# Both float32r parts of the input projection weights kept in DRAM from the first pass over the tokens

## The chip, the cores and the metric

The kernel runs on one core of one Trainium2 chip. The metric is device time in microseconds (us) from start to end of one execution. The core has a matrix engine (PE, with its weight loads PEld), a vector engine (DVE), an activation engine (ACT), GpSimd (POOL), a queue engine (SP) that issues most transfers, and 16 DMA engines that all queues share.

## What is computed

One layer of a hybrid encoder on 2112 tokens (2048 of a prompt, 64 of a running stream) of width 1024. All operands are float32.

```python
h    = rms_norm(x)
proj = einsum('btd,dc->btc', h, w_in)          # 1024 -> 5376 columns
A    = (bg * conv3_causal(cg * xin)) @ w_conv_out           # from the first 1536 columns
B    = rwkv7(proj[..., 1536:3328]) @ w_rwkv_out             # recurrence over tokens, state per head
m    = sigmoid(gate_A) * A + sigmoid(gate_B) * B            # gates: the last 2048 columns
x    = x + rms_norm(m @ w_o)
x    = x + rms_norm(swiglu(rms_norm(x)))
```

## The kernel before

Tokens lie on the free axis, features on the 128 partitions. Phase A does the input projection and the RWKV-7 recurrence; after it come the merge of the branches and the feed-forward part, which the change does not touch.

The projection's 5376 columns are 42 blocks of 128 (`w_in[c]`, 128x1024 floats, 512 KB each). The tokens are four quarters of 528, each done as two halves of 264. `PASSES` lists the work: a first pass with all 42 blocks for quarter 0, then passes with 28 blocks (quarter 1), 30 blocks (quarter 2) and 42 blocks (quarter 3), and at the end the 14 + 12 gate blocks that quarters 1 and 2 left over. So 168 units are done, and each block is fetched four times.

A float32 product is done as three float32r products: weights and activations are each split into a high part (rounded to float32r) and a low part (the rest), and `mm3` adds hi*hi, hi*lo and lo*hi. A unit takes 2 x 24 matmuls of 264 columns. Its weights come from `weights`: SP loads the block into `w_raw` (2 buffers), ACT writes `w_hi` (3 buffers) as a cast, DVE writes `w_lo` (3 buffers) as `w_raw - w_hi`. The load of the next unit is asked for at the start of a unit (`need`). ACT, DVE and SP each run their instructions strictly in the order written.

Between the projection's matmuls lie the three streams of the recurrence (`scan_prep`, `scan_solve`, `scan_chain`), which work on groups of 128 tokens: small matmuls, some 62 short DVE instructions per group that solve a triangular system (the tiles `tm`, `ti`, `al`), and round trips through DRAM (`asc`, `ttsc`). Two more jobs share the engines in phase A: `weight_sums`, which loads blocks of the feed-forward weights (`sw`), adds them on DVE and stores the sums (`us_s`, `ds_s`) for later, and the norm of the next quarter. A scheduler at build time sets the order in which each engine's instructions stand; it may bring a transfer forward where its queue would stand idle.

Of the kernel before, what the change touches and what calls it, by code (L numbers as in the profile page):

```python
# [16 lines left out]
P = 128  # L17
# [11 lines left out]
KT = D // P  # L29
# [56 lines left out]
class Trunk:  # L86
# [27 lines left out]
    def scratch(self):  # L114
        d = self.dram
        self.lo_s = d.tile([12, P, T], F32, name="lo_s")
        self.sg_s, self.a_s, self.g_s = self.lo_s[0:4], self.lo_s[4:8], self.lo_s[8:12]
        for nm in ("r", "v", "bv"):
            setattr(self, nm + "_s", d.tile([4, P, T], F32, name=nm + "_s"))
        self.ks_s = d.tile([12, P, T], F32, name="ks_s")  # L120
        self.gt_s = d.tile([16, P, T], F32, name="gt_s")
        self.cv_s = d.tile([4, P, T], F32, name="cv_s")
        self.yr_s = d.tile([4, P, T], F32, name="yr_s")
        self.x1_s = d.tile([KT, P, T], F32, name="x1_s")
        self.ds_s = d.tile([4, 4, P, FH * P], F32, name="ds_s")
        self.us_s = d.tile([4, NF, P, HK * P], F32, name="us_s")
        self.nb_s = d.tile([2, len(DOWN), HK, P, FB], F32, name="nb_s")
# [14 lines left out]
    def weights(self, src, kt=KT):  # L142

        nc = self.nc
        raw = self.wp.tile([P, KT, P], F32, name="w_raw", bufs=2)
        hi = self.wp.tile([P, KT, P], F32R, name="w_hi", bufs=WBUFS)
        lo = self.wp.tile([P, KT, P], F32R, name="w_lo", bufs=WBUFS)
        nc.sync.dma_start(out=raw[:, :kt], in_=src)
        nc.scalar.copy(out=hi[:, :kt], in_=raw[:, :kt])  # L149
        nc.vector.tensor_tensor(out=lo[:, :kt], in0=raw[:, :kt], in1=hi[:, :kt].bitcast(F32), op=ALU.subtract)  # L150
        return hi, lo

    def mm3(self, ps, w, r, kts, rk0=0, first=True, last=True, **kw):

# [122 lines left out]
        self.summing, self.sum_wait = self.weight_sums(), 24  # L277
        self.lora_in, self.conv_u, self.kf, self.bn = {}, {}, {}, {}

    def project(self, w, h, n):  # L280

        ps = self.mmps()
        for k in range(0, KT, KSTEP):
            if k:
                self.side_step()
                yield
            self.mm3(ps[:, :n], w, h, range(k, k + KSTEP), rk0=k, first=k == 0, last=k + KSTEP == KT)
        return ps

    def rwkv_unit(self, q, j, c, w, h):  # L290
# [3 lines left out]
        if 4 <= c < 8:  # L294
            a = pool.tile([P, NB], F32, name="ka", bufs=2)[:, :n]
            nc.sync.dma_start(out=a, in_=self.a_s[m, :, t0:t0 + n])
        ps = yield from self.project(w, h, n)
        x = pool.tile([P, NB], F32, name="psv", bufs=4)
        pr = pool.tile([P, NB + 2], F32, name="pr", bufs=2)
        for b, (s0, sn, sample) in enumerate(segments(t0, n)):  # L300
# [147 lines left out]
    def conv_unit(self, q, j, c, what, w, h):  # L448
        pool, nc = self.pa, self.nc
        t0, n = halves(q)[j]  # L450
        ps = yield from self.project(w, h, n)
        if what == 0:
            u = self.conv_u[j] = pool.tile([P, NB + 4], F32, name="u", bufs=2)
            for b, (s0, sn, sample) in enumerate(segments(t0, n)):
                b = s0 + 2 * b
                nc.scalar.copy(out=u[:, b + 2:b + 2 + sn], in_=ps[:, s0:s0 + sn])
        elif what == 1:
            u = self.conv_u[j]
            for b, (s0, sn, sample) in enumerate(segments(t0, n)):
                hist = self.u_hist_s if sample else self.u_hist  # L460
                b = s0 + 2 * b
                nc.gpsimd.tensor_copy(out=u[:, b:b + 2], in_=hist[:, c, :])
                nc.vector.tensor_tensor(out=u[:, b + 2:b + 2 + sn], in0=ps[:, s0:s0 + sn], in1=u[:, b + 2:b + 2 + sn], op=ALU.mult)
                nc.gpsimd.tensor_copy(out=hist[:, c, :], in_=u[:, b + sn:b + sn + 2])
        else:
            u = self.conv_u[j]
            y = pool.tile([P, NB], F32, name="prd", bufs=2)
            for b, (s0, sn, sample) in enumerate(segments(t0, n)):
                b = s0 + 2 * b
                ys = y[:, s0:s0 + sn]  # L470
                nc.scalar.activation(out=ys, in_=u[:, b:b + sn], func=AF.Copy, scale=self.cw[:, c, 0:1])
                for tap in (1, 2):
                    nc.vector.scalar_tensor_tensor(out=ys, in0=u[:, b + tap:b + tap + sn], scalar=self.cw[:, c, tap:tap + 1],
                                                   in1=ys, op0=ALU.mult, op1=ALU.add)
            nc.vector.tensor_tensor(out=y[:, :n], in0=ps[:, :n], in1=y[:, :n], op=ALU.mult)
            self.store(self.cv_s[c, :, t0:t0 + n], y[:, :n])

    def gate_unit(self, q, j, c, w, h):
        pool, nc = self.pa, self.nc
        t0, n = halves(q)[j]  # L480
        ps = yield from self.project(w, h, n)
        g = pool.tile([P, NB], F32, name="psv", bufs=4)
        nc.scalar.activation(out=g[:, :n], in_=ps[:, :n], func=AF.Sigmoid)
        nc.scalar.dma_start(out=self.gt_s[c, :, t0:t0 + n], in_=g[:, :n])

    def projections(self):


        def win(c):
            return lambda: self.weights(self.i["w_in"][c])  # L490
        flat, first = [], []
        for q, rw, conv, gates in PASSES:
            first.append(len(flat))
# [988 lines left out]
```

## Time and profile before

| | |
|---|---|
| median of 3 runs | 3306.06 us (3303.41 to 3307.27) |
| the profiled execution | 3308.43 us, of which span of the trace 3306.7 us |
| PE busy | 3133.8 us (95%) |
| DVE / ACT / POOL busy | 2475.3 / 1669.0 / 470.6 us |
| phase A | from 0 to about 1490 us |
| bytes moved by DMA | 699.52 MB, 212 GB/s on average |

PE is busy nearly all the time, so the kernel can only get shorter where PE waits or runs at a lower clock. A matmul's busy time says that PE was occupied, not that it ran at full speed; the granted clock stands beside it in the tables by stretch. Phase A is told apart below by its passes: 0 to 371 us, 371 to 622, 622 to 902, 902 to 1260, and the left-over gates to 1490.

### The profile page before, as it was taken

What the parts mean: (1) busy time and instruction counts of PE and PEld (TensorE: products, weight loads), DVE (VectorE), ACT (ScalarE), POOL (GpSimd) and SP (SyncE); (2) the same over time, 40 slices, a digit from 0 to 9 for tenths busy, and PEclk for the clock granted to TensorE, in tenths of its full rate; (3) what the DMA queues carried; (4) which work ended last, traced back from release to release, by engine and by line L of the source; (5) the groups of instructions that cost most, each with busy time, mean ns of one, the idle gap of its engine ahead of it and who ended that gap; (6) DMA issues with size and microseconds to landing.
All of it is one profiled execution on the core that took longest, in us unless ns stands there. A gap on an engine that the chain in (4) does not pass through costs nothing.

```text
span 3306.7 us, 64315 instructions
## 1 busy us (share of the span) xinstructions
PE 3133.8 (95%) x23060; PEld 3053.3 (92%) x23060; DVE 2475.3 (75%) x5325; ACT 1669.0 (50%) x3248; POOL 470.6 (14%) x885
## 2 busy tenths in 40 slices
PE   6999998999999999997999999999999999999997
PEld 5989898999989999996999999999999999899997
DVE  6875886878878767655486878886888876877767
ACT  6534654655575446543434444445645455444454
POOL 2400122122023200000010011210011200111100
PEclk9999999999999999998999999999999999999999
DMA  7788767766675656546475467778777877766675
GB/s 267 255 251 251 219 212 223 219 197 206 202 223 173 199 170 188 145 132 217 132 220 163 153 194 243 244 240 268 233 228 225 267 239 242 229 193 193 187 253 167
DMA packets 534833, 699.52 MB, mean 212 GB/s; under 512 B 112672, under 2 KB 368224, under 8 KB 534512
## 3 DMA queue, kind: packets, MB, share of 16 engines
q1 hardware_dynamic: 478592, 597.26, 59.2%
q0 software_dynamic: 24000, 67.61, 5.4%
q10 hardware_dynamic: 31920, 30.54, 2.7%
q8 instruction: 181, 2.97, 0.4%
q14 instruction: 140, 1.15, 0.1%
HBM read 522.10 MB, written 173.12 MB: 210 GB/s over the span
## 4 chain that ended last, share of the span: by engine, by line
issue 31%; PE 25%; POOL 3%; DMA 3%; DVE 2%; ACT 1%; SPq 0%; POOLq 0%; DVEq 0%; ACTq 0%
PE mm L136 23%; POOL tp_s L1228 2%; PE pu L136 1%; PE gy L136 1%; POOL x_s L1087 1%; POOL out_y L1087 1%; DMA r<-in_x 0%; DMA x_s<-r 0%; DVE f L1247 0%; DMA r<-x_s 0%; DMA w_raw<-in_w_up 0%; DVE w_lo L189 0%; DMA out_y<-r 0%; DVE rs L174 0%; PE tr L140 0%
## 5 line engine op out<-in xcount | busy, mean ns | idle before, releaser
L136 PE MATMUL mm<-h_hi,w_hi 128*128 128x264 f32 (+1 forms) x5112 | 1590.2, 311 | 58.7 <-ACT h_hi L188 21.9
L136 PE MATMUL mm<-h_lo,w_hi 128*128 128x264 f32 (+1 forms) x5112 | 1563.7, 306 | 4.4 <-DVE h_lo L217 3.7
L136 PE MATMUL mm<-h_hi,w_lo 128*128 128x264 f32 (+1 forms) x5112 | 1560.0, 306 | 5.6 <-DVE w_lo L150 5.5
L136 PEld LDWEIGHTS mm<-h_hi,w_hi 128*128 128x128 f32 x5112 | 975.7, 191 | 86.5 <-DVE f L1247 25.5
L136 PEld LDWEIGHTS mm<-h_lo,w_hi 128*128 128x128 f32 x5112 | 977.2, 191 | 10.3 <-DVE h_lo L217 4.9
L136 PEld LDWEIGHTS mm<-h_hi,w_lo 128*128 128x128 f32 x5112 | 977.1, 191 | 7.8 <-DVE w_lo L150 6.8
L188 ACT CAST w_hi<-w_raw 128x512 fp32r<-128x512 f32 (+1 forms) x810 | 486.2, 608 | 589.9 <-PE mm L136 434.8
L189 DVE TENSOR_TENSOR w_lo<-w_raw,w_hi 128x512 fp32r<-128x512 f32 (+1 forms) x810 | 540.9, 674 | 139.1 <-ACT w_hi L188 134.3
L136 PE MATMUL mm<-t_hi,w_hi 128*128 128x352 f32 x1116 | 360.7, 323 | 0.1
L136 PE MATMUL mm<-t_lo,w_hi 128*128 128x352 f32 x1116 | 358.4, 321 | 0.2 <-DVE t_lo L189 0.2
L136 PE MATMUL mm<-t_hi,w_lo 128*128 128x352 f32 x1116 | 358.3, 321 | 0.0
L150 DVE TENSOR_TENSOR w_lo<-w_raw,w_hi 128x1024 fp32r<-128x1024 f32 x168 | 206.7, 1232 | 113.0 <-ACT w_hi L149 109.4
L149 ACT CAST w_hi<-w_raw 128x1024 fp32r<-128x1024 f32 x168 | 175.8, 1048 | 140.4 <-PE mm L136 107.4
L136 PEld LDWEIGHTS mm<-t_lo,w_hi 128*128 128x128 f32 x1116 | 209.7, 188 | 1.0 <-DVE t_lo L189 0.6
L136 PEld LDWEIGHTS mm<-t_hi,w_hi 128*128 128x128 f32 x1116 | 209.4, 188 | 0.7 <-ACT t_hi L188 0.4
L136 PEld LDWEIGHTS mm<-t_hi,w_lo 128*128 128x128 f32 x1116 | 209.6, 188 | 0.0
L1228 POOL DMA_DIRECT2D tp_s<-f x231 | 125.0, 541 | 570.7 <-DVE f L1247 334.2
L189 DVE TENSOR_TENSOR t_lo<-d,t_hi 128x352 fp32r<-128x352 f32 x198 | 97.6, 522 | 80.1 <-ACT t_hi L188 79.7
L188 ACT CAST t_hi<-d 128x352 fp32r<-128x352 f32 x198 | 90.7, 486 | 111.4 <-DMA d<-tp_s 107.4
L1247 DVE TENSOR_TENSOR f<-mm,f 128x352 f32<-128x352 f32 x198 | 103.1, 521 | 49.1 <-PE mm L136 49.1
L761 DVE TENSOR_TENSOR ti<-ti,tm 128x60 f32<-128x60 f32 (+27 forms) x527 | 118.9, 226 | 7.7
L759 DVE TENSOR_TENSOR tm<-al,ti 128x60 f32<-128x60 f32 (+27 forms) x527 | 117.1, 222 | 8.5 <-DMA al<-asc 0.9
(199 smaller groups left out, 3761.7 us busy)
## 6 DMA issues: line engine op xcount, KB each, us to landing
w_raw<-in_w_in SPq DMA_DIRECT2D x168, 512.0 KB, 4.4
w_raw<-us_s SPq DMA_DIRECT2D x264, 256.0 KB, 3.0
w_raw<-in_w_up SPq DMA_DIRECT2D x198, 256.0 KB, 3.3
tp_s<-f POOLq DMA_DIRECT2D x231, 176.0 KB, 3.5
d<-tp_s SPq DMA_DIRECT2D x105, 352.0 KB, 3.9
w_raw<-ds_s SPq DMA_DIRECT2D x96, 256.0 KB, 3.7
sw<-in_w_up SPq DMA_DIRECT2D x88, 256.0 KB, 4.5
us_s<-sw SPq DMA_DIRECT2D x88, 256.0 KB, 3.6
```

The lines of the kernel that those rows point to most:

```text
L136: self.nc.tensor.matmul(out, lhsT, rhs, **kw)
L149: nc.scalar.copy(out=hi[:, :kt], in_=raw[:, :kt])
L150: nc.vector.tensor_tensor(out=lo[:, :kt], in0=raw[:, :kt], in1=hi[:, :kt].bitcast(F32), op=ALU.subtract)
L188: nc.scalar.copy(out=hi, in_=x)
L189: (eng or nc.vector).tensor_tensor(out=lo, in0=x, in1=hi.bitcast(F32), op=ALU.subtract)
L759: nc.vector.tensor_tensor(out=tv, in0=al[0:np_, u, u + 1:32].unsqueeze(1).broadcast_to([np_, k, m]), in1=ti[0:np_, 0:k, u:u + 1].broadcast ...
L761: nc.vector.tensor_tensor(out=tu, in0=tu, in1=tv, op=ALU.add)
L1087: (nc.sync if rows else nc.gpsimd).dma_start(out=dst[d, :, t0:t0 + n], in_=x)
L1228: nc.gpsimd.dma_start(out=self.tp_s[TP[op], i], in_=x)
L1247: nc.vector.tensor_tensor(out=out, in0=x, in1=y, op=op)
```

## The change

In the first pass a block is loaded and split as before, and when its unit begins both parts are stored to DRAM (`keep`, tiles `ws{c}_hi` and `ws{c}_lo`). In the other 126 units `input_weights` loads the two parts straight into `w_hi` and `w_lo`; `w_raw`, the cast on ACT and the subtraction on DVE are not used there. `project` is told the number of the block.

```diff
+        self.ws_s = [[d.tile([P, KT, P], F32, name=f"ws{c}_{s}") for s in ("hi", "lo")] for c in range(42)]
+        self.kept = {}
...
+    def input_weights(self, c):
+
+        nc = self.nc
+        if c not in self.kept:
+            self.kept[c] = False
+            return self.weights(self.i["w_in"][c])
+        w = [self.wp.tile([P, KT, P], F32R, name=f"w_{s}", bufs=WBUFS) for s in ("hi", "lo")]
+        for x, src in zip(w, self.ws_s[c]):
+            nc.sync.dma_start(out=x.bitcast(F32), in_=src)
+        return w
+
+    def keep(self, c, w):
+        if self.kept[c]:
+            return
+        self.kept[c] = True
+        for x, dst in zip(w, self.ws_s[c]):
+            self.nc.sync.dma_start(out=dst, in_=x.bitcast(F32))
...
-    def project(self, w, h, n):
+    def project(self, w, h, n, c):
 
         ps = self.mmps()
+        self.keep(c, w)
...
-        ps = yield from self.project(w, h, n)
+        ps = yield from self.project(w, h, n, 12 + c)
...
-            return lambda: self.weights(self.i["w_in"][c])
+            return lambda: self.input_weights(c)
```

The other two callers of `project` pass their block's number in the same way.

On SP, in the middle of the first pass, the rows before are loads of blocks (`w_raw`), loads and stores of `weight_sums` (`sw`, `us_s`) and stores of results (`v_s`, `bv_s`):

```order
L148 DMA w_raw<-in_w_in 128x1024
L609 DMA us_s<-sw 128x512 x2
L602 DMA sw<-in_w_up 128x512 x2
L148 DMA w_raw<-in_w_in 128x1024
L602 DMA sw<-in_w_up 128x512 x2
L380 DMA v_s<-psv 128x264
L380 DMA bv_s<-bn 128x264
L609 DMA us_s<-sw 128x512
L148 DMA w_raw<-in_w_in 128x1024
```

The same place now, with the two stores of parts behind each load:

```order
L150 DMA w_raw<-in_w_in 128x1024
L317 DMA ka<-lo_s 128x264
L171 DMA ws_hi<-w_hi 128x1024
L171 DMA ws_lo<-w_lo 128x1024
L401 DMA r_s<-psv 128x264
L317 DMA ka<-lo_s 128x264
L150 DMA w_raw<-in_w_in 128x1024
L171 DMA ws_hi<-w_hi 128x1024
L171 DMA ws_lo<-w_lo 128x1024
```

The stores have moved in, and the scheduler has put the transfers of `weight_sums` later: ahead of the first load of parts there stand 28 loads `sw` and 24 stores of sums in the new order.

On SP, early in the second pass, before (`r_s`, `ks_s` are stores of results, `ka` and `sg` loads for them and for the recurrence):

```order
L380 DMA r_s<-psv 128x264
L148 DMA w_raw<-in_w_in 128x1024
L650 DMA sg<-lo_s 128x4x128
L380 DMA r_s<-psv 128x264
L602 DMA sw<-in_w_up 128x512
L380 DMA ks_s<-ks 128x3x264
L296 DMA ka<-lo_s 128x264
L148 DMA w_raw<-in_w_in 128x1024
```

and now:

```order
L401 DMA r_s<-psv 128x264
L163 DMA w_hi<-ws_hi 128x1024
L163 DMA w_lo<-ws_lo 128x1024
L401 DMA r_s<-psv 128x264
L630 DMA us_s<-sw 128x512 x4
L401 DMA ks_s<-ks 128x3x264
L163 DMA w_hi<-ws_hi 128x1024
L163 DMA w_lo<-ws_lo 128x1024
```

One load per unit has become two, and these wait until PE has done with the buffer that they fill, where the load of `w_raw` waited until DVE had read the raw block before.

On DVE, in the second pass, between the short instructions of the triangular solve (`tm`, `ti`), before:

```order
L369 RECIPROCAL hf<-hf 128x264
L759 TENSOR_TENSOR tm<-al,ti 128x2x26
L370 SCALAR_TENSOR_TENSOR ks<-psv,cpack,hf 128x264
L150 TENSOR_TENSOR w_lo<-w_raw,w_hi 128x1024
L829 TENSOR_TENSOR stmp<-pu,st_107 64x256 x2
L832 TENSOR_TENSOR st_108<-stmp,cc 64x4x64 x2
L761 TENSOR_TENSOR ti<-ti,tm 128x2x26
```

and now:

```order
L390 RECIPROCAL hf<-hf 128x264
L209 TENSOR_TENSOR p_5519<-prd,p_5518 128x264
L391 SCALAR_TENSOR_TENSOR ks<-psv,cpack,hf 128x264
L850 TENSOR_TENSOR stmp<-pu,st_191 64x256 x2
L853 TENSOR_TENSOR st_192<-stmp,cc 64x4x64 x2
L780 TENSOR_TENSOR tm<-al,ti 128x3x23
```

The subtraction that stood ahead of the state's update (`stmp`, `st`) is gone, as it is from every unit after the first 42.

## Rows read from the trace of the kernel before

**Rows 1.** The page, costliest groups: busy and mean ns, idle time before them and its releaser
```profile
L150 DVE TENSOR_TENSOR w_lo<-w_raw,w_hi 128x1024 fp32r<-128x1024 f32 x168 | 206.7, 1232 | 113.0 <-ACT w_hi L149 109.4
L149 ACT CAST w_hi<-w_raw 128x1024 fp32r<-128x1024 f32 x168 | 175.8, 1048 | 140.4 <-PE mm L136 107.4
```

**Rows 2.** Busy time by stretch: pass 0, pass 1, pass 2, pass 3, left-over gates
```profile
core 0: us, PE busy (x) PEld busy (x) DVE busy (x) ACT busy (x) POOL busy (x), PEclk, DMA share, GB/s
...
20.00:371.00 351.00, 325.02 (x2711) 313.45 (x2711) 254.95 (x554) 185.48 (x347) 63.42 (x113) 0.96 0.78 249
371.00:622.00 251.00, 230.55 (x1961) 221.62 (x1960) 190.69 (x441) 137.17 (x274) 54.53 (x102) 0.94 0.70 214
622.00:902.00 280.00, 266.10 (x2436) 253.92 (x2436) 227.66 (x596) 160.63 (x317) 57.97 (x112) 0.98 0.69 208
902.00:1260.00 358.00, 342.38 (x3082) 326.17 (x3081) 271.26 (x739) 194.88 (x392) 71.89 (x152) 0.95 0.64 188
1260.00:1490.00 230.00, 225.58 (x2105) 217.01 (x2104) 147.46 (x382) 118.38 (x209) 10.56 (x14) 1.00 0.53 155
```

**Rows 3.** What PE waited for from 371 to 1490 us: total, times, longest
```profile
PE pa L136 <- DVE v L704: 12.1, 9, 2.3
PE tr L140 <- DVE aq L715: 7.6, 4, 4.0
PE mm L136 <- ACT bn L188: 5.1, 2, 3.4
PE pu L136 <- DVE d L775: 4.9, 5, 2.3
PE pu L136 <- DVE aa L715: 4.0, 4, 1.8
...
PE mm L136 <- DVE w_lo L150: 2.5, 2, 2.0
PE tr L140 <- DMA v<-v_s: 1.4, 1, 1.4
```

**Rows 4.** What DVE, then ACT waited for from 371 to 1490 us
```profile
DVE w_lo L150 <- ACT w_hi L149: 84.9, 42, 6.6
...
DVE d L775 <- DMA tinv<-ttsc: 10.1, 6, 3.5
...
ACT w_hi L149 <- PE mm L136: 70.1, 45, 3.9
...
ACT w_hi L149 <- DMA w_raw<-in_w_in: 20.1, 13, 5.2
```

**Rows 5.** Two stretches of 50 us with much and little DVE work, columns as in rows 2
```profile
950.00:1000.00 50.00, 43.56 (x351) 41.29 (x352) 47.17 (x115) 38.28 (x71) 15.63 (x28) 0.93 0.77 247
1200.00:1250.00 50.00, 49.98 (x496) 48.02 (x496) 30.47 (x91) 20.36 (x33) 0.49 (x3) 1.00 0.52 154
```

**Rows 6.** DMA from 20 to 371 us: packets, then issues by line, KB each, us to landing
```profile
DMA packets 70248, 87.49 MB, mean 249 GB/s; under 512 B 13629, under 2 KB 47821, under 8 KB 70210
...
w_raw<-in_w_in SPq DMA_DIRECT2D x42, 512.0 KB, 4.7
us_s<-sw SPq DMA_DIRECT2D x65, 256.0 KB, 3.6
sw<-in_w_up SPq DMA_DIRECT2D x64, 256.0 KB, 4.8
```

**Rows 7.** The busiest stretches of the DMA engines in phase A, columns as in rows 2
```profile
10.00:20.00 10.00, 1.80 (x4) 0.75 (x4) 8.98 (x10) 7.73 (x16) 5.74 (x7) 1.00 1.00 324
50.00:60.00 10.00, 8.01 (x55) 6.87 (x54) 2.92 (x7) 6.16 (x17) 1.00 (x4) 1.00 0.98 342
50.00:100.00 50.00, 41.45 (x291) 38.98 (x291) 30.56 (x52) 33.66 (x66) 12.52 (x23) 0.93 0.90 306
```

**Rows 8.** The loads of `w_raw` on SP: issue ns min/median/max, then landing of all 168
```profile
L148 SPq DMA_DIRECT2D w_raw<-in_w_in x168: 327/346/1601, 2.3 to 1469.5; - x168
...
DMA to landing us min/median/max: 3.2/4.4/7.8
```

**Rows 9.** What SP waited for from 371 to 1490 us
```profile
SPq L148 <- DVE w_lo L150: 115.4, 38, 13.5
SPq L148 <- DVE ti L761: 61.3, 24, 9.2
```

**Rows 10.** PE at the start of pass 1, in order of time; then the stretch after it
```profile
381.63 0.51 PE L136 MATMUL mm<-bn,w_hi 128*128 128x264 f32 x2 [3.35 <-ACT bn L188]
...
382.00:390.00 8.00, 8.00 (x49) 7.65 (x48) 6.20 (x20) 6.11 (x14) 0.37 (x2) 0.57 0.53 164
```

More of the change, by code (lines that the diff above doesn't have):

```diff
@@ L450, in conv_unit @@
         t0, n = halves(q)[j]
-        ps = yield from self.project(w, h, n)
+        ps = yield from self.project(w, h, n, c + 4 * (0, 2, 1)[what])
         if what == 0:
@@ L480, in gate_unit @@
         t0, n = halves(q)[j]
-        ps = yield from self.project(w, h, n)
+        ps = yield from self.project(w, h, n, 26 + c)
         g = pool.tile([P, NB], F32, name="psv", bufs=4)
```

## The prediction, written before the changed kernel was run

> **What bounds the kernel now.** I read the table by stretch first. Its columns to compare are the length of a stretch, PE's busy time and the granted clock [rows 2]. PE is the bound in every pass, but not quite: in the 1119 us from 371 to 1490 it is idle for 251 - 230.55, 280 - 266.10, 358 - 342.38 and 230 - 225.58, together 54.4 us. The clock takes more: 0.94, 0.98, 0.95 and 1.00 granted mean that 15.1 + 5.6 + 17.9 + 0 = 38.6 us of full-speed time are missing. So 93 us is all that work off PE can give back in the passes from which the conversions go. The rest of the kernel, 1816 us after phase A, is not touched.
>
> The waits of PE say who ends that idle time: DVE's scan operands (`v`, `aq`, `d`, `aa`) and once in a while a low weight part; the five DVE rows shown make 31.1 us, the ACT row 5.1, the transfer row 1.4 [rows 3]. No single one is long. DVE is the second busiest engine, 76, 81, 76 and 64% of the four stretches, and where it is fullest PE loses most: with 47.17 of 50 us of DVE work PE is busy 43.56 at clock 0.93, with 30.47 it is busy 49.98 at 1.00 [rows 5].
>
> The third reading is the DMA share. In pass 0, where the change adds stores, the engines are already 0.78 busy at 249 GB/s [rows 2]; there, transfers are the second bound.
>
> **The change, part by part.** The sum is made against the profiled execution, 3308.4 us (1.7 us of it outside the span), which is 2.4 us above the median of the three runs.
>
> *Conversions removed.* 126 of 168 casts and subtractions go. A subtraction takes 1.232 us and a cast 1.048 [rows 1], so 126 x 1.232 = 155 us leave DVE and 126 x 1.048 = 132 us leave ACT. More goes than the busy time. ACT stands 70.1 us in this stretch waiting for PE to release the buffer that a cast is to fill and 20.1 us for the raw block, and everything behind the cast on ACT (evacuations of PSUM for the projection and the scan) stands with it; DVE stands 84.9 us behind those casts [rows 4]. Without them DVE is held 155 + 85 = 240 us less out of 1119, and its busy share falls from 837 to 682 us, 75 to 61%. None of this is PE's time, so it counts only through the 93 us. The lower bound of the gain is nothing: if PE's waits are the latency of a chain that goes PE, ACT, DVE and back, a shorter queue does not help. The upper bound is 31 + 5 us of waits that end on DVE and ACT, with all 38.6 us of the clock: 75 us. The two stretches of rows 5 speak for a good part, since the difference in DVE work between them (16.7 us in 50) is what separates 6.4 us of idle time from none; but the fullest stretch is also a pass's start, with its norm and decay work. I take half of the idle time, 27 us, and 15 us of the clock: **-42 us**.
>
> *Stores added in pass 0.* 84 stores of 512 KB are 44.0 MB beside the 87.49 MB that pass 0 moves now [rows 6]. The order also moves work out: 64 loads and 65 stores of `weight_sums` fall into this stretch now [rows 6], and in the new order 52 stand ahead of the first load of parts, which itself stands some units before the end of the pass, so I count 60. The 69 that go, at 262 KB, take 18.1 MB away (with some 35 additions on DVE). What is left to move is 113.4 MB, 323 GB/s if pass 0 is to stay at 351 us. Bounds from rows: 342 GB/s in the best 10 us, at share 0.98 [rows 7], would need 332 us and cost nothing. The mix of today moves 249 / 0.78 = 319 GB/s per fully busy second [rows 2]; if the engines can't be kept over the 0.90 of the busiest 50 us [rows 7], that is 287 GB/s, 395 us, +44. The same 50 us moved 306 GB/s: 371 us, +20. I take less than that row gives, **+12 us**, because the new packets are longer than the mean of the mix (4 KB rows), because weights are asked for two units ahead, and because the passes behind have some room to catch up.
>
> The Trainium skill, "DMA: Bandwidth & Descriptors", section "Where 436 GB/s comes from", puts the ceiling of the 16 engines at 435 GB/s. By that figure the 113.4 MB would take 261 us, this term would be nothing, and the sum would give 3282 us. The trace disagrees for this mix: with the engines busy without a gap it shows 324 GB/s.
>
> Casts and subtractions stay in pass 0, and each store waits on SP for its part. That wait is not new: the load of the block after next waited for the same subtraction, since it needs the raw buffer. The buffer of a part is now also held until its store has landed, some 4 us after the subtraction, while two more units lie ahead of its reuse; hidden.
>
> *Loads of parts in passes 1 to 3.* A unit's weights used to be ready 1.05 + 1.23 us after PE had released their buffer, and the raw block had landed by then. Now the transfer starts there: 0.35 us of issue and 4.4 us to landing for the first part [rows 8], and the second behind it with 0.52 MB at 319 GB/s, 1.6 us: some 6.4 us, 4 us later than before. In the middle of a pass a buffer is released about two units ahead of its use, a unit takes some 251 / 28 = 9 us [rows 2], and that hides it. At the start of a pass it does not: blocks 24 and 25 and the small matrices hold all three buffers over both halves, and the next two blocks are asked for with little more than half a unit and the small products between. That is two places in each of three passes. With landings of 4.4 us the cover about suffices; with the longest of 7.8 [rows 8] PE waits some 3 us, and such a wait brings the low clock: a wait of 3.35 us is followed by 8 us at 0.57, 3.4 us lost [rows 10]. Bounds 0 and 6 x 6.4 = 38 us; taken near the low end, as the median landing asks: **+8 us**.
>
> *Queues.* Everything behind a load of parts on SP (scan loads, stores of results, `ka`) waits with it until PE releases a buffer. Before, SP stood 115.4 + 61.3 us for the subtraction and for the DVE work that kept the subtraction waiting [rows 9]; that goes, and a like wait for PE comes. 210 more issues at 0.35 us are 73 us on SP in 1490, where SP has those waits to spare; hidden. The DMA engines are busy 176 + 193 + 229 + 122 = 720 us of the 1119 now [rows 2]; 126 x 0.524 MB and the 18.1 MB from pass 0 are 84 MB, at 319 GB/s 264 us: 0.88 in place of 0.64. Landings grow (4.7 us in pass 0 against 4.4 over all blocks [rows 6, 8]), and DVE's waits for round trips with them, 10.1 us for `tinv` now [rows 4]. Bounds 0 and 30, three times that row; taken **+10 us**.
>
> Sum: -42 + 12 + 8 + 10 = -12 us. 3308.4 - 12 = 3296 for a profiled execution, **3294 us** as a median.
>
> **The rivals.**
>
> *Pass 0 is bound by its transfers (slower).* Place: 20 to 371 us. At 287 GB/s the term is +44 in place of +12, and the time 3294 + 32 = 3326. With the other terms at -24 it ends on the slow side once the loss there is over 31 us, that is under 113.4 / 382 = 297 GB/s. For it: pass 0 needs 323 GB/s on average, and the busiest 50 us moved 306. Against: stretches of 10 us moved 324 and 342 [rows 7].
>
> *The relief is small (no change).* If PE's waits are the scan's own latency, the gain is some 30 us and the extra transfers take it all: 3306. For it: the waits are many and short, none over 4.0 us [rows 3]. Against: rows 5.
>
> *The relief is nearly whole.* -75 with the same costs: -45, 3261. For it: 240 us less on DVE's queue against 31 us of waits that end on DVE. Against: starts of passes have their idle time for other reasons as well.
>
> **How the numbers follow.** Forecast 0.34 (its own range 3278 to 3299), the larger relief 0.16, no change 0.18, pass 0 bound 0.32. A change within 0.2%, 6.6 us, is about what a measurement can't tell from none; so faster 0.50, same 0.18, slower 0.32. The range reaches from the larger relief, 3258, to pass 0 at 287 GB/s with the starts of passes at some 27 us in place of 8, 3345; below and above I leave 1 in 10 each.
>
> **What would show it.** Pass 0 ends near 383 us with a DMA share of 0.9 or more; if it ends by 371, the store term was nothing, and if after 402, the forecast falls. In passes 1 to 3 the rows of `w_lo` on DVE and `w_hi` on ACT are gone, DVE is near 61%, PE's idle time near 27 us plus what the starts of passes add, and the clock nearer to 1.00. New rows of PE waiting for a transfer of `w_hi` or `w_lo` should stand at starts of passes alone. The prediction is wrong if such waits run through the passes, or if the scan's waits stay at their size with DVE at 61%.

## The result and the profile after

The changed kernel takes 3459.27 us (median of 4 runs, 3448.68 to 3472.5) against 3304.97 before: the ratio is 1.0469, with a 95% interval of 1.0443 to 1.0495. It is slower by 154 us, on the other side of the forecast and outside its range. The profiled execution of it has a span of 3450.5 us against 3306.7.

From the page, here are the row of busy times, the row of the DMA packets and the rows of two groups of loads (KB each, median us to landing):

```profile
PE 3200.6 (93%) x23060; PEld 3103.6 (90%) x23060; DVE 2375.3 (69%) x5199; ACT 1549.3 (45%) x3119; POOL 426.5 (12%) x885
...
DMA packets 565072, 809.62 MB, mean 235 GB/s; under 512 B 116032, under 2 KB 371584, under 8 KB 564752
...
w_hi<-ws_hi SPq DMA_DIRECT2D x126, 512.0 KB, 5.4
w_lo<-ws_lo SPq DMA_DIRECT2D x126, 512.0 KB, 6.0
```

Work has gone from DVE and ACT (100 and 120 us less busy, where the removed instructions had been counted at 155 and 132), and 110 MB of transfers have come. PE is busy for longer, although it runs the same 23060 matmuls: it runs more of them at the lower clock.

To compare pass by pass, a pass is counted from ACT's first evacuation of a product with the small matrices (`ks`) to the same point of the next pass, and pass 3, with the left-over gates behind it, to the last sigmoid of a gate. All tables below use these marks. The table of busy time by stretch for the kernel before (columns in the first line; the last row is the rest of the kernel):

```profile
core 0: us, PE busy (x) PEld busy (x) DVE busy (x) ACT busy (x) POOL busy (x), PEclk, DMA share, GB/s
37.40:384.00 346.60, 321.24 (x2717) 310.08 (x2717) 250.86 (x553) 181.67 (x340) 61.21 (x109) 0.97 0.80 253
384.00:634.50 250.50, 231.80 (x1967) 223.23 (x1966) 191.80 (x447) 137.99 (x279) 52.78 (x101) 0.94 0.70 216
634.50:921.40 286.90, 274.06 (x2470) 260.64 (x2469) 230.44 (x606) 161.64 (x317) 56.59 (x115) 0.97 0.69 206
921.40:1503.90 582.50, 562.63 (x5190) 539.13 (x5189) 409.16 (x1087) 308.26 (x585) 81.03 (x157) 0.98 0.58 171
1503.90:3306.70 1802.80, 1729.35 (x10660) 1707.90 (x10658) 1364.75 (x2583) 853.71 (x1680) 204.46 (x377) 0.99 0.68 217
```

and for the changed kernel:

```profile
36.50:431.70 395.20, 344.49 (x2737) 326.12 (x2736) 240.54 (x540) 174.32 (x332) 48.81 (x109) 0.91 0.83 278
431.70:709.60 277.90, 244.86 (x1977) 233.54 (x1976) 166.20 (x400) 115.42 (x254) 41.38 (x103) 0.89 0.79 250
709.60:1027.00 317.40, 281.69 (x2421) 265.73 (x2421) 212.62 (x580) 128.53 (x280) 46.96 (x110) 0.93 0.77 242
1027.00:1653.80 626.80, 584.71 (x5209) 555.28 (x5208) 361.69 (x1050) 250.52 (x527) 70.58 (x161) 0.95 0.78 244
1653.80:3450.50 1796.70, 1730.38 (x10660) 1710.89 (x10658) 1366.35 (x2583) 855.24 (x1680) 204.51 (x377) 0.99 0.69 217
```

Every pass lost: 48.6, 27.4, 30.5 and 44.3 us. The rest of the kernel did not (-6.1). In each pass PE is idle for longer (50.7 against 25.4 us in pass 0, 33.0 against 18.7 in pass 1) and has a lower clock (0.91 against 0.97, 0.89 against 0.94). Of the 102 us that passes 1 to 3 lost, 59 are idle time of PE and 43 are a longer busy time for about the same matmuls. DVE is down to 60% in pass 1 (166.20 of 277.90), and the pass is longer all the same. The DMA share, which I had expected at 0.88 in passes 1 to 3, stands at 0.77 to 0.79, and the rate at 242 to 250 GB/s.

PE's waits in passes 1 to 3, 431.7 to 1653.8 us (total, times, longest), answer to [rows 3]:

```profile
PE mm L138 <- DMA w_hi<-ws_hi: 17.5, 5, 7.5
PE mm L138 <- DVE acc L204: 14.3, 5, 4.5
PE pa L138 <- DVE v L725: 14.1, 8, 3.9
PE tr L142 <- ACT ysq L881: 9.1, 5, 2.8
...
PE mm L138 <- DMA w_lo<-ws_lo: 4.8, 7, 1.2
```

Waits for parts make 22.3 us, in 12 places. They do not stand at starts of passes alone, as had been foreseen: the longest comes just ahead of the mark of pass 2, the next two in the middle of pass 1 (start in us, length, then the wait before it in brackets):

```profile
516.27 0.56 PE L138 MATMUL mm<-h_hi,w_hi 128*128 128x264 f32 x1 [4.58 <-DMA w_hi<-ws_hi]
582.88 0.56 PE L138 MATMUL mm<-h_hi,w_hi 128*128 128x264 f32 x1 [3.53 <-DMA w_hi<-ws_hi]
697.90 0.59 PE L138 MATMUL mm<-h_hi,w_hi 128*128 128x264 f32 x1 [7.54 <-DMA w_hi<-ws_hi]
```

The scan's operands (`v`), the norm's sums (`acc`) and results on their way out (`ysq`) are waited for as well, with DVE and ACT less busy than before. What held those up these rows do not say.

One more thing moved that the diff doesn't show. These are the loads of `weight_sums` for the feed-forward's first weights up to the end of pass 0, first before, then after:

```profile
sw<-in_w_up SPq DMA_DIRECT2D x68, 256.0 KB, 4.9
```

```profile
sw<-in_w_up SPq DMA_DIRECT2D x32, 256.0 KB, 5.2
```

Of the 136 loads of sums the passes now hold 32, 24, 28 and 52, where they held 68, 24, 24 and 20.

### The profile page after: what moved, and what is told of

Its sections match the earlier page's. It is cut to its first block, busy times and chain, and to the rows that moved or that the text cites. A ratio compares the mean times of both kernels' runs of the same rounds, so it can differ in the third digit from the quotient of the medians.

```text
span 3450.5 us, 64225 instructions
## 1 busy us (share of the span) xinstructions
PE 3200.6 (93%) x23060; PEld 3103.6 (90%) x23060; DVE 2375.3 (69%) x5199; ACT 1549.3 (45%) x3119; POOL 426.5 (12%) x885
## 4 chain that ended last, share of the span: by engine, by line
PE 42%; issue 29%; DVE 11%; DMA 10%; POOL 3%; ACT 3%; SPq 1%; POOLq 0%; ACTq 0%; DVEq 0%
PE mm L138 36%; PE pu L138 3%; DMA w_lo<-ws_lo 2%; DVE ti L782 2%; DVE tm L780 1%; POOL tp_s L1249 1%; PE gy L138 1%; DMA lo_s<-ks 1%; DMA w_raw<-in_w_in 1%; DVE hf L390 1%; DVE acc L204 1%; PE pa L138 1%; POOL x_s L1108 1%; DVE psv L328 1%; DVE sw L626 1%
## 5 line engine op out<-in xcount | busy, mean ns | idle before, releaser
L138 PE MATMUL mm<-h_hi,w_hi 128*128 128x264 f32 (+1 forms) x5112 | 1603.3, 314 | 81.6 <-ACT h_hi L208 21.3
L138 PEld LDWEIGHTS mm<-h_hi,w_hi 128*128 128x128 f32 x5112 | 990.1, 194 | 110.3 <-DVE f L1268 24.4
L138 PEld LDWEIGHTS mm<-h_hi,w_lo 128*128 128x128 f32 x5112 | 987.2, 194 | 21.2 <-DVE w_lo L152 12.6
L138 PEld LDWEIGHTS mm<-h_lo,w_hi 128*128 128x128 f32 x5112 | 992.3, 194 | 8.1 <-DVE h_lo L237 3.9
L504 ACT ACTIVATE psv<-mm 128x264 f32<-128x264 f32 x128 | 49.8, 389 | 225.7 <-PE mm L138 210.7
L780 DVE TENSOR_TENSOR tm<-al,ti 128x60 f32<-128x60 f32 (+27 forms) x527 | 124.3, 236 | 18.4 <-DMA ti<-in_eye 5.8
L782 DVE TENSOR_TENSOR ti<-ti,tm 128x60 f32<-128x60 f32 (+27 forms) x527 | 126.7, 240 | 12.9
L328 DVE SCALAR_TENSOR_TENSOR psv<-pr,cpack,psv 128x264 f32<-128x264 f32 (+2 forms) x126 | 58.8, 474 | 78.0 <-ACT psv L327 57.1
```

Source lines behind the costliest of these rows:

```text
L138: self.nc.tensor.matmul(out, lhsT, rhs, **kw)
L328: nc.vector.scalar_tensor_tensor(out=x[:, s0:s0 + sn], in0=pr[:, b:b + sn], scalar=self.mu[:, c:c + 1], in1=x[:, s0:s0 + sn], op0=ALU.mult ...
L780: nc.vector.tensor_tensor(out=tv, in0=al[0:np_, u, u + 1:32].unsqueeze(1).broadcast_to([np_, k, m]), in1=ti[0:np_, 0:k, u:u + 1].broadcast ...
L782: nc.vector.tensor_tensor(out=tu, in0=tu, in1=tv, op=ALU.add)
```

## The experiments

Two theories stood against each other. **Bytes**: the added transfers hold each other and all other transfers up, in pass 0 by the stores, later by the second part and by the sums that were pushed there. **Order and waits**: SP is one in-order queue; loads of parts stand in it until PE releases a buffer, stores until a conversion is done, and what is behind them comes late. All kernels stand in the table at the end of this section; each was timed beside the kernel before on the same chip, and its ratio is to that time.

**One half at a time.** *Stores alone*: the later units load the raw block again.

```diff
-        if c not in self.kept:
-            self.kept[c] = False
-            return self.weights(self.i["w_in"][c])
...
+        self.kept.setdefault(c, False)
+        return self.weights(self.i["w_in"][c])
```

> The parts are stored in the first pass, but the later passes load the raw block and convert as before. The changed kernel lost 48.6 us in its first pass and 102 us in the passes behind it. If the loss of the first pass is made by the stores alone, this kernel loses about 45 to 55 us there and nothing behind: 3305 + 50 = 3355 us. If instead the first pass is slow because the build placed the other transfers differently once later loads depend on its stores, it loses under 20 us: 3305 to 3325.

*Loads alone*: `keep` stores block 24 only, and all later units load its parts (so their products use the wrong weights).

```diff
-        for x, src in zip(w, self.ws_s[c]):
+        for x, src in zip(w, self.ws_s[24]):
...
-        if self.kept[c]:
+        if self.kept[c] or c != 24:
```

> Only the parts of block 24 are stored, and every later unit loads those two parts, whatever its block (so its products are with the wrong weights; transfers, buffers and waits are those of the changed kernel). If the loads make their own loss, the passes behind the first lose about 100 us and the first nothing: 3305 + 100 = 3405 us. If the passes behind are late only because the first pass pushed its transfers of the weight sums into them, they lose under 30 us: 3305 to 3335.

*One load*: as the loads alone, with one part in the place of both (it leaves the low part out).

```diff
-        w = [self.wp.tile([P, KT, P], F32R, name=f"w_{s}", bufs=WBUFS) for s in ("hi", "lo")]
-        for x, src in zip(w, self.ws_s[c]):
-            nc.sync.dma_start(out=x.bitcast(F32), in_=src)
-        return w
+        w = self.wp.tile([P, KT, P], F32R, name="w_hi", bufs=WBUFS)
+        nc.sync.dma_start(out=w.bitcast(F32), in_=self.ws_s[24][0])
+        return w, w
```

> As the kernel with the loads alone, but each later unit loads one part and uses it for both (the low part is left out), so that it moves no more bytes than the kernel before and converts nothing. If the bytes of the second part make the loss, this kernel is as fast as before or faster by the relief of DVE and ACT: 3265 to 3305 us. If the loss comes from where the loads stand (they are asked for only once PE has released their buffer, in one in-order queue with the results of DVE and ACT), half of the 100 us or more stays: 3355 to 3405.

*Four buffers*: `WBUFS` is 4.

> The changed kernel with four buffers for each part in place of three. If the loss comes from loads that start late behind PE's release, a buffer comes free a unit earlier (9 us) and most of the 102 us of the later passes comes back, while the first pass keeps its 49: 3350 to 3400 us. If the bytes make the loss, the fourth buffer moves it by 15 us at most: 3445 to 3465.

Stores alone cost 33 us (1.0103, interval 1.0081 to 1.0126): pass 0 is 49.1 us longer, as in the changed kernel, and passes 1 and 2 are 10.6 and 2.6 us shorter. Loads alone cost 16 (1.0051), the second answer of its expectation, not the 100 us. So the halves make 49 us and the whole 154: something in the whole is in neither half. One load gained 36 us (0.9889), 41 of it in passes 1 to 3; a fourth buffer gave back 15 us. Both speak for bytes.

**What joins the halves.** *Same block*: the changed kernel, each later unit loading block 24's parts (first pair of lines of the diff of the loads alone).

> The changed kernel, with every later unit loading the stored parts of block 24 in place of its own (wrong weights; the order of the instructions on every engine, the bytes and the buffers are those of the changed kernel). Stores alone cost 33 us and loads alone 16, both together 154. If the two together are dear because a load must wait for its own block's store, or because 42 different blocks are read, this kernel takes 3355 to 3380 us. If it is the bytes or the order, it takes as long as the changed kernel, 3445 to 3470.

*Short sums*: every load, addition and store of `weight_sums` a quarter as long; the feed-forward part, which would use the sums, loads blocks of its weights in their place.

```diff
-                    nc.sync.dma_start(out=w[i, j], in_=x)
+                    nc.sync.dma_start(out=w[i, j][:, :1], in_=x[:, :1])
...
-                nc.sync.dma_start(out=dst(sm), in_=w[k].rearrange("p k c -> p (k c)"))
+                nc.sync.dma_start(out=dst(sm)[:, :P], in_=w[k][:, 0])
```

> The changed kernel, with the transfers and additions of the weight sums cut to a quarter of their length (same number of transfers; the products that use the sums are wrong, and the later phase reads blocks of the same size from the weights themselves). The changed kernel holds 104 of the 136 loads of the sums in the passes that also load parts; the kernel with the loads alone holds 68. If transfers of sums and loads of parts collide by their bytes, 60 us or more of the 154 comes back: 3380 us or less. If the number of issues and their waits on SP's one queue make the loss, it stays within 25 us of the changed kernel: 3435 to 3465.

*Loads on ACT*, *stores on POOL*: `nc.scalar` in `input_weights`, `nc.gpsimd` in `keep`, in place of `nc.sync`.

> The changed kernel, with the loads of parts issued by ACT's queue in place of SP's (ACT waited for the same releases of PE in the kernel before, ahead of its casts). If the loss of the later passes is SP's one in-order queue, in which the loads stand behind waits for DVE and POOL and hold others up, most of their 102 us comes back: 3350 to 3390. If the DMA engines are full, the same bytes from another queue take as long: 3440 to 3480, and ACT's evacuations behind the waits can add to it.

> The changed kernel, with the stores of parts issued by POOL's queue in place of SP's. If the 49 us of the first pass come from the place of the stores in SP's queue, they shrink to under 15 and the time is 3410 or less. If they come from the bytes, the first pass stays at 385 to 400 us and the time within 15 us of the changed kernel.

Same block took 3460: neither the wait for an own store nor 42 addresses matter. Short sums took 3349, 110 us less than the changed kernel at the same number of transfers. DVE is 58 us less busy in it as well, and what part of the 110 that made was not tried. Loads from ACT's queue took 3463, as long as from SP's. That is a poor test of the queue, since its build moved the sums: their loads stand 60, 44 and 0 in passes 1 to 3, against 24, 28 and 52 in the changed kernel. Its passes 1 and 3:

```profile
428.40:733.80 305.40, 243.23 (x1937) 231.40 (x1936) 183.13 (x443) 112.90 (x251) 41.58 (x103) 0.89 0.90 293
...
1054.80:1661.30 606.50, 571.83 (x5203) 547.74 (x5202) 322.90 (x995) 250.51 (x528) 66.70 (x159) 0.96 0.69 205
```

Pass 1 moved 293 GB/s and lost 54.9 us. Pass 3 lost 24.0 us without any sums in it and at 205 GB/s: that loss is not one of bytes. ACT's own work behind waits of the loads is a candidate that was not tried.

Stores on POOL were a surprise: 3383, with pass 0 still worse (407.3 us), but passes 1 and 2 at 240.7 and 285.7, better than before. The build had put 72 loads of sums back into pass 0; passes 1 and 2 were left with 9 and 11. No other first pass has the DMA engines busy for as large a share:

```profile
45.70:453.00 407.30, 342.58 (x2711) 329.22 (x2711) 251.59 (x557) 180.03 (x340) 94.72 (x191) 0.90 0.95 324
```

So where the sums stand decides. In the next runs they are held in place by an edge on SP's queue, which gives the 32, 24, 28 and 52 of the changed kernel to any other one:

```diff
-        nc.sync.dma_start(out=raw[:, :kt], in_=src)
+        self.last_load = nc.sync.dma_start(out=raw[:, :kt], in_=src).ins
...
-            next(self.summing, None)
+            with self.tc.issue_after(self.last_load):
+                next(self.summing, None)
```

In kernels that load parts, those loads set `last_load` too.

**The sums held in place**, in the kernel with the loads alone, in the kernel before, and in the one with stores on POOL; and **sums on POOL**, where the changed kernel issues all their transfers from POOL's queue.

> The kernel with the loads alone, with the transfers of the weight sums held on SP's queue behind the weight load of the same unit, so that they spread over the passes as in the changed kernel (28 of 136 loads of sums ahead of the first load of parts, 60 there before). No added stores. If loads of parts and sums in one pass are what costs in passes 1 to 3, they lose their 27 + 30 + 44 us here too, and the time is 3380 to 3410. If the stores are needed for that loss, it stays near the 3327 of the loads alone.

> The kernel before, with the sums held behind the weight loads in the same way, with no stores and no loads of parts. If sums that come later cost by themselves, it loses in the later passes: 3330 or more. If they cost only beside loads of parts, it is within 15 us of the kernel before: 3290 to 3320.

> Stores of parts on POOL's queue, and the sums spread as in the changed kernel. With stores on POOL and 64 loads of sums in the first pass, that pass took 407 us and moved 132 MB at 324 GB/s. With the sums spread it has some 112 MB to move. If the DMA engines bind there, it takes 346 us and loses nothing; if a store costs in itself (its wait, its buffer), it stays at 385 or more. The passes behind lose their 100 us if sums and loads of parts collide: 3400 to 3410 in all by the first answer, 3445 or more by the second.

> The changed kernel with the loads and stores of the weight sums issued by POOL's queue; the stores and loads of parts stay on SP. If what costs in passes 1 to 3 is SP's one queue, in which sums, loads of parts and results stand in line, most of the 102 us comes back: 3350 to 3385. If it is the bytes on the DMA engines, it stays at 3440 to 3475.

The loads alone with the sums spread lose 70 us where they lost 16 (1.0217; at 3379 a little under the range given). The kernel before with the sums spread loses nothing: it gains 0.66% (0.9934, interval 0.9911 to 0.9958). So sums are dear only beside loads of parts. With stores on POOL and sums spread, pass 0 took 384.1 us for 114 MB, 297 GB/s: between the two answers, better than the 407.3 with more sums in it, and short of 324 GB/s; its passes 1 to 3 lost 80 us, and so the time, 3431, lies between the answers too. With the sums on POOL the build ran nearly all of them (124 of 136 loads) in pass 0, which then took 522 us, and so the median stayed at 3463 for another reason than expected. The passes it freed are the best of witnesses: they load both parts of every block and hold no sums.

```profile
821.30:1096.30 275.00, 263.83 (x2406) 251.15 (x2406) 193.80 (x555) 131.28 (x285) 45.30 (x114) 0.99 0.74 225
1096.30:1663.20 566.90, 554.28 (x5210) 532.87 (x5209) 325.72 (x998) 247.89 (x523) 66.35 (x158) 0.99 0.73 222
```

Pass 2 is 11.9 and pass 3 15.6 us shorter than before, at clock 0.99 and 222 to 225 GB/s. One load with the sums spread, below, has the same relief and nearly the same bytes, with sums in the place of the second parts, and takes 276.6 and 563.2 us. So the second parts, late as they are asked for, cost no more than other transfers of their size.

**Bytes without lateness, lateness without bytes.** *Extra load*: the kernel before with sums spread, and a dead load of 512 KB with each later unit.

```diff
+    def input_weights(self, c):
+        if c in self.seen:
+            spare = self.wp.tile([P, KT, P], F32, name="spare", bufs=2)
+            with self.tc.issue_after(self.last_load):
+                self.nc.sync.dma_start(out=spare, in_=self.i["w_in"][c])
+        self.seen.add(c)
+        return self.weights(self.i["w_in"][c])
...
-            return lambda: self.weights(self.i["w_in"][c])
+            return lambda: self.input_weights(c)
```

> The kernel before with the sums spread (3290 us), and one more load of 512 KB for each of the 126 later units, into a spare buffer that nothing reads and that waits for nothing of PE. It moves in each pass what the kernel with the loads alone and spread sums moves (3379 us), converts as before, and has its weights as early as before. If the added bytes beside the sums make the loss, it loses some 80 us in passes 1 to 3: 3350 to 3380. If the loss is that parts are asked for only when PE releases their buffer, it stays at 3285 to 3310.

*One load, sums spread*:

> One load for each later unit, used for both parts (the low part left out), and the sums spread. No more bytes than before, no conversions, but loads that are asked for when PE releases their buffer, beside sums. If the bytes decide, it gains as with the sums in the first pass: 3255 to 3285. If the late asking decides, it loses half or more of what the kernel with both loads and spread sums lost: 3325 or more.

*Short stores*: the stores alone, a quarter as long.

```diff
-            self.nc.sync.dma_start(out=dst, in_=x.bitcast(F32))
+            self.nc.sync.dma_start(out=dst[:, :2], in_=x[:, :2].bitcast(F32))
```

> The kernel with the stores alone (3344 us, first pass 395.7), with each store cut to a quarter of its length; the same 84 stores on SP, with the same waits, and the same hold on the buffers. If the bytes of the stores cost, the first pass takes 346 to 360 us and the time is 3300 to 3318. If the stores' waits on SP or the hold on the buffers cost, it stays at 380 or more and 3330 to 3345.

These three weigh most. Passes 1 to 3 of the kernel before with sums spread, and of the one with the extra load:

```profile
373.80:615.40 241.60, 227.90 (x1974) 218.92 (x1973) 195.32 (x445) 145.66 (x282) 51.91 (x103) 0.97 0.73 224
615.40:910.00 294.60, 279.49 (x2464) 264.88 (x2464) 235.64 (x605) 162.33 (x320) 57.70 (x114) 0.95 0.71 212
910.00:1490.70 580.70, 560.22 (x5194) 536.34 (x5193) 423.99 (x1120) 311.72 (x587) 80.00 (x157) 0.99 0.66 198
```

```profile
370.60:636.70 266.10, 240.34 (x1965) 228.84 (x1963) 197.55 (x444) 144.11 (x281) 47.41 (x101) 0.91 0.80 253
636.70:962.70 326.00, 286.28 (x2472) 269.10 (x2472) 241.82 (x611) 163.19 (x319) 53.18 (x114) 0.93 0.76 237
962.70:1602.20 639.50, 585.85 (x5196) 555.23 (x5192) 432.83 (x1115) 316.06 (x595) 79.79 (x158) 0.94 0.75 237
```

Nothing reads the extra block; yet the passes are 24.5 + 31.4 + 58.8 = 114.7 us longer, more than the 80 expected, with clock and rate as in the changed kernel. Part of the way to PE can be seen in the landings. First the raw block's load with the sums spread (KB each, median us) and PE's waits for what is made of it, then the two loads with the extra one, then PE's first two waits of that kernel:

```profile
w_raw<-in_w_in SPq DMA_DIRECT2D x122, 512.0 KB, 4.4
```

```profile
PE mm L136 <- ACT w_hi L149: 3.5, 2, 2.1
...
PE mm L136 <- DVE w_lo L150: 2.5, 5, 1.0
```

```profile
spare<-in_w_in SPq DMA_DIRECT2D x122, 512.0 KB, 5.8
w_raw<-in_w_in SPq DMA_DIRECT2D x122, 512.0 KB, 5.5
```

```profile
PE mm L137 <- ACT w_hi L150: 23.8, 10, 9.0
PE mm L137 <- DVE w_lo L151: 11.3, 15, 2.4
```

The raw block lands 1.1 us later in the median, and PE waits 35 us for its conversions where it waited 6. That is 29 us of the 70 by which PE's idle time grew; the other 45 of the 115 us are a longer busy time at the lower clock. The extra loads also put 126 more issues on SP's queue, and a short dead load was not run. Short sums and short stores, which keep the number of transfers and lose their bytes, and the sums spread on POOL, which take 272 issues off SP and gain nothing, speak for the bytes.

One load with sums spread has the late asking without the bytes, and gains: 3251 (0.9823, interval 0.9802 to 0.9845), 38.6 us under the kernel before with sums spread. Its passes 1 to 3:

```profile
367.90:606.50 238.60, 224.04 (x1967) 217.01 (x1966) 167.18 (x415) 111.28 (x247) 40.01 (x101) 0.96 0.73 224
606.50:883.10 276.60, 266.59 (x2469) 253.16 (x2467) 208.20 (x581) 133.10 (x290) 48.21 (x114) 0.99 0.75 223
883.10:1446.30 563.20, 554.61 (x5208) 532.94 (x5206) 351.81 (x1049) 246.96 (x522) 68.56 (x158) 0.99 0.69 208
```

Short stores take 3306, with pass 0 at 346.9 us: the same 84 stores, with the same waits, cost nothing at a quarter of the length, although 48 loads of sums stand in that pass where the stores alone have 32.

**Two last questions.** *Subtraction on POOL*: `nc.gpsimd` for `lo` in `weights`, sums spread, to have the relief without any transfer.

> The kernel before with the sums spread, and the subtraction of each projection weight on POOL in place of DVE: 207 us leave DVE and no bytes are added. If DVE's queue holds PE up, as the term of the conversions assumed, it gains 15 to 30 us on 3290: 3260 to 3275. If POOL's slower subtraction (884 ns for 264 columns, so an estimate of 3.4 us for a block) holds the weights up or keeps POOL's other work waiting, it is 3290 or more.

*Sums spread on POOL*: the sums from POOL's queue, held behind POOL's own last instruction of the unit.

> The changed kernel with the loads and stores of the weight sums on POOL's queue, held there behind POOL's own work of the same units, so that they spread over the passes as in the changed kernel; stores and loads of parts stay on SP. Bytes by pass are those of the changed kernel. In every kernel whose transfers of these passes all came from SP, passes 1 to 3 moved no more than about 250 GB/s. If that ceiling is SP's line of waits, a second queue lifts it, and passes 1 to 3 lose under 40 us in place of 102: 3400 or less. If the transfers hold each other up on the engines, whoever issues them, the time is 3440 to 3475.

The subtraction on POOL took 3430: a different loss (told at the end). The sums from a second queue at their old places took 3471, with passes 1 and 2 at 268.1 and 312.0 us and 257 and 246 GB/s. In pass 3 part of the 648.8 us may be POOL's own waiting. So taking the sums off SP's line does not bring the time back. The Trainium skill, "DMA: Bandwidth & Descriptors", section "Issuing engines are not separate DMA queues", says that DMAs of whichever engine run on the same 16 engines, so that issuing from several saves only the time of issue; the kernel with the sums spread on POOL, at 3471 against 3459, agrees with it.

All runs, by pass (change of its length in us against the kernel before / MB moved in it, as length times GB/s), with the ratio to the kernel before:

| kernel | us | ratio | pass 0 | pass 1 | pass 2 | pass 3, gates |
|---|---|---|---|---|---|---|
| before | 3305 | 1 | 346.6 us / 88 | 250.5 / 54 | 286.9 / 59 | 582.5 / 100 |
| changed | 3459 | 1.0469 | +48.6 / 110 | +27.4 / 69 | +30.5 / 77 | +44.3 / 153 |
| stores alone | 3344 | 1.0103 | +49.1 / 109 | -10.6 / 60 | -2.6 / 61 | +2.2 / 113 |
| short stores | 3306 | 0.9991 | +0.3 / 87 | -2.3 / 55 | +0.7 / 60 | +1.3 / 109 |
| loads alone | 3327 | 1.0051 | -1.0 / 89 | -10.3 / 60 | +0.8 / 68 | +28.4 / 149 |
| one load | 3274 | 0.9889 | +6.7 / 89 | -15.7 / 55 | -7.3 / 62 | -17.8 / 94 |
| four buffers | 3444 | 1.0414 | +38.3 / 110 | +19.1 / 70 | +26.5 / 76 | +52.0 / 153 |
| same block | 3460 | 1.0457 | +49.1 / 110 | +27.8 / 70 | +33.8 / 77 | +46.9 / 153 |
| short sums | 3349 | 1.0121 | +26.5 / 99 | +3.3 / 60 | +1.6 / 65 | +9.3 / 134 |
| loads on ACT | 3463 | 1.0468 | +45.0 / 110 | +54.9 / 89 | +34.1 / 85 | +24.0 / 124 |
| stores on POOL | 3383 | 1.0223 | +60.7 / 132 | -9.8 / 59 | -1.2 / 69 | +21.3 / 147 |
| sums on POOL | 3463 | 1.0463 | +175.7 / 157 | +4.8 / 63 | -11.9 / 62 | -15.6 / 126 |
| sums spread on POOL | 3471 | 1.0477 | +54.4 / 113 | +17.6 / 69 | +25.1 / 77 | +66.3 / 152 |
| *sums spread:* before | 3290 | 0.9934 | -10.0 / 71 | -8.9 / 54 | +7.7 / 62 | -1.8 / 115 |
| loads alone | 3379 | 1.0217 | -12.9 / 72 | +15.1 / 67 | +25.8 / 78 | +38.7 / 153 |
| extra load | 3399 | 1.0263 | -13.2 / 73 | +15.6 / 67 | +39.1 / 77 | +57.0 / 152 |
| one load | 3251 | 0.9823 | -15.8 / 70 | -11.9 / 53 | -10.3 / 62 | -19.3 / 117 |
| stores on POOL | 3431 | 1.0359 | +37.5 / 114 | +14.8 / 67 | +29.8 / 78 | +35.5 / 153 |
| subtraction on POOL | 3430 | 1.0365 | +20.9 / 71 | +18.9 / 54 | +27.3 / 62 | +54.0 / 117 |

The rest of the kernel, which none of these edits means to change, differs from the kernel before by -6.4 to +8.6 us between these traces; so a few us in the table say nothing.

Read down a column without the last line, and divide the bytes by the length that the pass had before: that is the rate the pass would need to lose nothing. Where passes 1 and 2 need up to 241 GB/s they are at most 7.7 us longer than before, and often shorter; where they need 264 or more, they lose 14.8 us or more, whoever issues the transfers. Pass 3 loses 9.3 us at 230 and 21 or more from 253 on, pass 0 26.5 at 286. The exception is pass 3 with the loads on ACT, told above. The rate that a pass did move says less: pass 1 of the loads alone moved 248 GB/s and was 10.3 us shorter than before, where the changed kernel moved 250 and was 27.4 us longer.

```profile
382.90:623.10 240.20, 226.97 (x1979) 217.27 (x1979) 157.02 (x402) 114.77 (x248) 39.47 (x99) 0.96 0.80 248
```

## Why the prediction was wrong

*Conversions removed, -42: right in size.* Without added bytes the kernel gains 36 us (one load against before) or 39 (the same with sums spread in both). The lighter queues of DVE and ACT do reach PE, at the size taken from the idle time and the clock.

*Stores in pass 0, +12: mis-sized.* They cost 49 us. The bytes were right (110 MB against the 113.4 counted); the rate was not. I set the needed 323 GB/s against the best stretches [rows 7] and gave the engines the benefit of the doubt; pass 0 ran at 278 GB/s. The rival that put pass 0 at 287 GB/s, +44, had this term right. Short stores show that it is bytes, and not the stores' waits. The 49 us stand after sums had left the pass: against the kernel before with the same 32 loads of sums in pass 0 the stores alone cost 59.1.

*Loads at the starts of passes, +8: small as foreseen, not told apart from nothing, and not at the starts alone.* Loads of parts with sums spread lose 82.6 us in passes 1 to 3 against the kernel before with sums spread (24.0 + 18.1 + 40.5). With the relief of 39 put back that is 121, and the extra load makes 114.7. Some 7 us would remain for late asking, if these effects add up. The same sum made with the medians of the whole kernels (88.6 + 38.6 - 109.0) gives 18, so the remainder is known only as small. Of PE's 22.3 us of waits for parts, 10 stand just ahead of the marks of passes 2 and 3 and 11 in the middle of pass 1.

*Queues, +10, with an upper bound of 30: this is the step that failed.* I divided the new bytes by the 319 GB/s of a fully busy second, found a share of 0.88 under 1, and let the rest be hidden, with three times the wait for `tinv` as the most that longer landings could cost. Passes 1 to 3 of the changed kernel lost 102 us with the relief in them, so the transfers took some 141, an estimate from the two. Extra load puts 115 of these down to the second part beside the sums. Both had been counted, the pushed sums too (84 MB in all, and 86 came); what was wrong is that they were priced at next to nothing. The wait behind the bound, 10.1 us in [rows 4], did grow to three times its size in these passes:

```profile
DVE d L796 <- DMA tinv<-ttsc: 32.5, 8, 18.1
```

But the loss does not follow it: in passes 1 to 3 of the loads alone it was 29.0 us, and they lost 18.9. Sums moved alone cost nothing there (-3.0 us over the three passes), nor do the second parts alone with the DMA at 225 GB/s. It takes both.

The fault in both steps is one: share and rate were read as room. A mean share of 0.64 did not say that 0.24 more was free. PE needs single transfers in time, and at shares of 0.75 to 0.80 they land later: by 1.1 us for a raw block in the run with the extra load, with 35 us of waits for what is made of it, and a clock of 0.91 to 0.94 in these passes. By the prediction's own signs it was wrong: DVE is at 61% in passes 1 to 3, and PE's waits for the scan did not shrink (`v` 14.1 us against 12.1).

A slip on the side: the range's lower end, 3258, is put down to the larger relief, whose sum is 3261.

What stays open: 22.6 us of the 102 in passes 1 to 3, by which the changed kernel is worse than its loads alone with sums at about the same places (the order on the other engines differs); and why PE already loses where a pass needs 264 GB/s, when passes, lengthened ones, did move 293 and 324. It may be bursts in which all 16 engines are full, or the chain of the scan with its round trips longer; no run here tells them apart. Against one of these trips, the load of `al`, speaks that it landed after 6.1 us in passes 1 to 3 of the changed kernel (3.5 before) and after 6.7 in passes 2 and 3 with the sums on POOL, which lost nothing.

## What to carry to other kernels

Before trading computation for transfers, add up the bytes that each pass would have to move, those that the scheduler will push into it too, and divide by the pass's present length. For passes 1 to 3 that was 267 GB/s here, (215 + 84) MB in 1119 us, and these runs lost time from some 230 to 264 on, far below the best stretch. That border was read from this kernel; another will have its own. To learn whether a transfer costs by its bytes or by its place, add a dead one, or shorten the one in doubt and keep its waits. Here the better step was the opposite one: holding the sums' transfers in an even spread over the passes, without keeping any parts, gave 3290 us, 0.66% under the kernel before (interval of the ratio 0.9911 to 0.9958).

## What the runs showed of the hardware

DVE operations with both operands in SBUF became slower when POOL took over the subtraction. Here are the rows of two DVE operations (busy us and mean ns stand behind the count), first with the subtraction on DVE and then on POOL:

```profile
L307 DVE SCALAR_TENSOR_TENSOR psv<-pr,cpack,psv 128x264 f32<-128x264 f32 x69 | 35.0, 509 | 14.2 <-ACT psv L306 8.3 <-POOL pr_hist L305 3.8 <-POOL pr L303 1.6
...
L830 DVE TENSOR_TENSOR stmp<-pu,st 64x256 f32<-64x256 f32 x58 | 24.3, 419 | 15.4 <-PE pu L136 14.4
```

```profile
L307 DVE SCALAR_TENSOR_TENSOR psv<-pr,cpack,psv 128x264 f32<-128x264 f32 x70 | 46.3, 664 | 25.9 <-ACT psv L306 19.0 <-POOL pr_hist L305 4.2 <-issue 1.3
...
L830 DVE TENSOR_TENSOR stmp<-pu,st 64x256 f32<-64x256 f32 x60 | 25.1, 418 | 15.1 <-PE pu L136 14.2
```

The first grew from 509 to 664 ns; the second, which reads one operand from PSUM, stayed at 419 and 418. The Trainium skill, "SBUF — State Buffer", section "SBUF: two separate sides", says that DVE instructions with two SBUF inputs and GpSimd instructions that read SBUF take turns on a shared pair of ports; these rows agree. POOL's own operations did not become slower: its sum `bn` took 1042 ns in the mean with the subtraction on DVE and 837 with it on POOL. The subtraction itself took 2.39 us on POOL in the median (1.23 on DVE), and PE waited for it only 6.7 us in passes 1 to 3. Its longer waits were for DVE (`v` 23.0, `yt` 21.2, `aq` 15.3 us), so that I put most of the 140 us that this kernel lost against the one with the sums spread down to a slower DVE; that was argued, and not tried by itself.

One more point is of the build and not of the chip: it brings transfers forward on a queue that has little else to do. With the sums on POOL's queue it placed 124 of their 136 loads in pass 0, and that pass grew to 522 us at 300 GB/s.
